# A convolutional FFN on one core: the first chunk's halves in the other order with x1 turned between them, the last group by pairs of blocks, the samples' halves summed by a product

## Chip, core and metric

The kernel runs on one core of one Trainium2 chip. The metric is the device time of one launch in microseconds (us): the kernel before has a median of 1758.8 us in 3 runs (1758.32 to 1759.49). The core has five engines with a static order of instructions each: TensorE (PE in the profile), VectorE (DVE), ScalarE (ACT), GpSimd (POOL) and SyncE (SP), which here issues most DMAs. An instruction waits on its engine until what it reads is there and what it overwrites is free; everything behind it on that engine waits too.

## What is computed

One layer of a hybrid decoder, for 256 tokens of a prompt and 64 tokens of 8 samples (8 each), D_MODEL = 2048, D_FF = 5632, all in float32:

```python
def decoder_layer(x, ssm_state, ssm_conv_state, ffn_conv_state, p):
    ...                                     # mix: chunk MLP and SSD, then w_out
    x = x + rms_norm(mix, p["norm_mix_post"])
    f, new_ffn_conv = conv_ffn(rms_norm(x, p["norm_ffn_pre"]), ffn_conv_state,
                               p["ffn_w_up"], p["ffn_conv_w"], p["ffn_conv_b"], p["ffn_w_down"])
    x = x + rms_norm(f, p["norm_ffn_post"])

def conv_ffn(h, conv_state, w_up, conv_w, conv_b, w_down):
    up = h @ w_up                           # 2048 -> 2 x 5632
    up, new_conv = causal_depthwise_conv(up, conv_state, conv_w, conv_b)   # 3 taps along the tokens
    g, u = jnp.split(up, 2, axis=-1)
    return (jax.nn.gelu(g, approximate=True) * u) @ w_down, new_conv
```

Only the FFN, its two norms and the last sum are touched. Below, x1 is x after the mix part and r3 is the reciprocal root of x1's mean square, one number for each token.

## The kernel before

**Layout.** Activations stand with features on the 128 partitions and the 320 tokens (256 prompt, 64 sample) as columns. TensorE multiplies in a rounded format, so every product of the prompt is made as three: high times high, weight's high times activation's low, weight's low times activation's high (L135 to L137 in the up-projection, L1465 in the down-projection). A group of weights (128x1024) is loaded by SP into `wraw`, ScalarE casts the high part `whi` (L124), VectorE subtracts for the low part `wlo` (L125); there are three buffers of each, so a cast waits until TensorE is done with an older one. For weights of the down-projection the lines are L1480 (cast) and L1481 (subtraction). The samples' rows of the down-projection are made with unsplit values (`pms`, `pds`, L1472).

**Up-projection.** It goes by NG = 11 groups g of 512 columns of the gate half (half 0) and 512 of the other half (half 1): `ffn_up(g)`. `project` runs 4 PSUM tiles of 128 columns over 16 feature blocks. Behind each tile stands `evac`: VectorE scales it by r3 into `pad` (L1334, L1335), ScalarE makes the first tap of the convolution (L1341), VectorE the other two (L1343), ScalarE gelu for half 0 (L1348), VectorE the product with the gate, `a` for the prompt and `a_s` for the samples (L1351, L1352). `Parts.cut` splits blocks of `a`, and sums of blocks (s1 to s4), into high (ScalarE, L398) and low (VectorE, L399) parts. Group 0 begins before r3 is known: `ps_one`, then `ps_other` are its last two tiles, and after a few of ps_one's products the token sums give r3 (L275 to L282), which TensorE spreads over all partitions (`spread`, L298) and ScalarE copies (L300).

**Down-projection.** The 512 rows of `w_down` that belong to group ck are chunk ck. `down_steps(ck)` is a generator that runs in the background of `ffn_up(ck+1)`: at each `yield` a slab of the up-projection goes on. For each half m of the 2048 output columns it makes seven products instead of eight (Strassen and Winograd's scheme; blocks b11, b12, b21, b22 of the weights, their sums t1 to t4 on POOL, L1510), each in a PSUM tile `pm` of 12 matmuls of 512 columns. `taken_in` then moves the tile to one of seven running sums per half: for chunk 0 by a ScalarE copy (L1457), later by a VectorE add (L1459). The sums of half 0 lie in `in_mix` (in the memory of x1, tag acc_mix), those of half 1 in `in_fp`. After chunk 9, `together(m)` adds the seven to the four blocks f that they stand for (L1555). The last chunk (10) is done by `down_plain` without the scheme (`pd`), some weights being held (`held_w`) for a second use; `others(n)` loads x1 back in rows of tokens (`load_x1`), `done` is `one_block` (square, and product with the norm's gain), and after a token block's four columns' blocks `whole` makes the root and the output (L1655 to L1687). Token blocks are c = 0 and 1 (prompt) and 2 (samples, whose columns lie in two halves on 128 partitions).

**x1 in rows.** The last sum needs x1 with tokens on partitions. `to_rows(i)`, called four times at the start of chunk 0, transposes a quarter of x1 in blocks of 32 on VectorE (L1440) and stores it by four DMAs on SP (L1443). Its buffers in_turn have the tags ohi and olo, which are also those of `a` and `s`. Since in_mix takes x1's memory, the first copy into in_mix comes after the four turns.

**Order.** A scheduler puts the instructions of each engine in a fixed order when the program is built: by the order of the code, by priorities (`first()` raises by 200000, weights by 100000) and by explicit `issue_after`.

## Time and profile before

| | us |
|---|---|
| median of 3 runs (lowest, highest) | 1758.8 (1758.32, 1759.49) |
| the profiled execution | 1760.49 |
| its span (first to last instruction) | 1758.8 |
| TensorE busy in it | 1728.8 (98%) |
| VectorE busy | 1355.5 (77%) |
| ScalarE busy | 881.2 (50%) |
| GpSimd busy | 692.6 (39%) |
| TensorE clock granted, mean | 0.992 |

The profile is of one execution; its clock is the share of full speed that TensorE was granted. In rows of the timeline the first number is the start, the second the duration in us; what stands in brackets is how long the instruction waited and for what. Rows of waits give the engine, the waiting tile and line, what ended the wait, then the total, the count and the longest. In rows by stretches each engine's busy time and count stand in the order TensorE, VectorE, ScalarE, GpSimd and SyncE, then the clock, the DMA engines' share and their GB/s.

### The profile page before, as it was taken

The page shows a single profiled execution, that of the slowest core. Times are in us where ns is not written, and L with a number is a line of the kernel's source. Part 1 is how long each engine was busy: PE and PEld are TensorE (multiplying, and loading weights), DVE is VectorE, ACT ScalarE, POOL GpSimd, SP SyncE. Part 2 cuts the span into 40 slices and gives each one's busy share as a digit, 9 for nine tenths or more (in the row PEclk, how much of TensorE's full clock was granted, in tenths as well). Part 3 has the DMA queues.
Part 4 walks back from the last instruction along what each step waited for, and adds up shares of the span by engine and source line. Part 5 has one row for each costly group of instructions (what it writes and reads, how often), then busy time and mean ns, then how long its engine had stood idle before and what let it go on. Part 6 is the DMA issues. An engine that isn't in the chain of part 4 may idle for free.

```text
span 1758.8 us, 29958 instructions
## 1 busy us (share of the span) xinstructions
PE 1728.8 (98%) x11221; PEld 1609.3 (92%) x11221; DVE 1355.5 (77%) x2127; ACT 881.2 (50%) x1276; POOL 692.6 (39%) x1006
## 2 busy tenths in 40 slices
PE   9999999999999999999989999999999999999986
PEld 9999999999999999999978898888888888888864
DVE  6549863657879787879867788879797979797885
ACT  6344544334656564645545444444444545454543
POOL 2432230000432324021345556565555556565534
PEclk9999999999999999999999999999999999999998
DMA  8776665555776677655665444455545454545442
GB/s 251 227 236 183 181 180 151 157 168 188 221 213 215 208 230 215 220 172 164 209 182 156 147 149 144 155 172 163 167 150 164 153 159 151 163 156 160 146 146 96
DMA packets 212962, 310.60 MB, mean 177 GB/s; under 512 B 22224, under 2 KB 112976, under 8 KB 212496
## 3 DMA queue, kind: packets, MB, share of 16 engines
q1 hardware_dynamic: 195424, 279.50, 52.0%
q0 software_dynamic: 6176, 13.87, 2.7%
q10 hardware_dynamic: 11216, 15.31, 2.5%
q8 instruction: 88, 1.44, 0.3%
q14 instruction: 58, 0.48, 0.1%
HBM read 285.00 MB, written 22.32 MB: 175 GB/s over the span
## 4 chain that ended last, share of the span: by engine, by line
PE 96%; DVE 2%; issue 1%; DMA 1%; ACT 0%; POOL 0%; DVEq 0%; ACTq 0%; SPq 0%; POOLq 0%
PE ps L135 20%; PE ps L137 20%; PE ps L136 20%; PE pm L1465 11%; PE pd L135 4%; PE pd L137 4%; PE pd L136 4%; PE pms L1472 4%; PE pd L1465 1%; PE y_ps L1088 1%; PE ps_v L135 1%; PE ps_v L136 1%; PE ps_v L137 1%; DVE wlo L125 0%; PE yo_ps L1003 0%
## 5 line engine op out<-in xcount | busy, mean ns | idle before, releaser
L135 PE MATMUL ps<-h_hi,whi 128*128 128x320 f32 x2428 | 750.1, 309 | 1.0 <-ACT whi L124 1.0
L137 PE MATMUL ps<-h_hi,wlo 128*128 128x320 f32 x2428 | 748.4, 309 | 0.5 <-DVE wlo L125 0.3
L136 PE MATMUL ps<-h_lo,whi 128*128 128x320 f32 x2428 | 748.5, 308 | 0.0
L125 DVE TENSOR_TENSOR wlo<-wraw,whi 128x1024 fp32r<-128x1024 f32 (+2 forms) x395 | 489.9, 1241 | 155.3 <-ACT whi L124 153.5
L124 ACT CAST whi<-wraw 128x1024 fp32r<-128x1024 f32 (+2 forms) x394 | 406.1, 1031 | 378.2 <-PE ps L136 139.9
L135 PEld LDWEIGHTS ps<-h_hi,whi 128*128 128x128 f32 x2428 | 455.8, 188 | 10.3 <-issue 1.3
L136 PEld LDWEIGHTS ps<-h_lo,whi 128*128 128x128 f32 x2428 | 456.0, 188 | 6.1
L137 PEld LDWEIGHTS ps<-h_hi,wlo 128*128 128x128 f32 x2428 | 455.5, 188 | 1.3 <-DVE wlo L125 1.3
L1481 DVE TENSOR_TENSOR wlo<-b,whi 128x1024 fp32r<-128x1024 f32 x120 | 153.8, 1281 | 79.7 <-ACT whi L1480 79.4
L1480 ACT CAST whi<-b 128x1024 fp32r<-128x1024 f32 x120 | 125.6, 1046 | 162.8 <-PE ps L136 153.8
L1510 POOL TENSOR_TENSOR b<-b,b 128x256 f32<-128x256 f32 x160 | 183.1, 1168 | 0.0
L135 PE MATMUL pd<-ohi,whi 128*128 128x320 f32 x448 | 138.7, 310 | 0.0
L137 PE MATMUL pd<-ohi,wlo 128*128 128x320 f32 x448 | 138.3, 309 | 0.0
L136 PE MATMUL pd<-olo,whi 128*128 128x320 f32 x448 | 138.3, 309 | 0.0
L1510 POOL TENSOR_TENSOR b<-b,t 128x256 f32<-128x256 f32 x80 | 75.0, 947 | 96.9 <-PE pms L1472 96.9
L1346 POOL COPY ptf<-pad 128x2 f32<-128x2 f32 x88 | 42.2, 480 | 166.9 <-DVE pad L1334 166.2
L1510 POOL TENSOR_TENSOR t<-b,b 128x256 f32<-128x256 f32 x80 | 89.7, 1151 | 23.3 <-DMA b<-in_ffn_w_down 16.1
L135 PEld LDWEIGHTS pd<-ohi,whi 128*128 128x128 f32 x448 | 84.1, 188 | 0.6
L136 PEld LDWEIGHTS pd<-olo,whi 128*128 128x128 f32 x448 | 84.1, 188 | 0.3
L137 PEld LDWEIGHTS pd<-ohi,wlo 128*128 128x128 f32 x448 | 84.1, 188 | 0.0
L248 DVE TENSOR_TENSOR acc_mix<-acc_mix,pd 128x320 f32<-128x320 f32 (+1 forms) x113 | 53.6, 477 | 28.0 <-PE pd L137 27.7
L1472 PE MATMUL pms<-b,a_s 128*64 128x512 f32 x320 | 73.1, 598 | 0.0
(407 smaller groups left out, 2496.1 us busy)
## 6 DMA issues: line engine op xcount, KB each, us to landing
wraw<-in_ffn_w_up SPq DMA_DIRECT2D x176, 512.0 KB, 4.5
wraw<-in_w_in SPq DMA_DIRECT2D x132, 512.0 KB, 3.9
b<-in_ffn_w_down SPq DMA_DIRECT2D x80, 512.0 KB, 4.5
wraw<-in_w_out SPq DMA_DIRECT2D x64, 512.0 KB, 3.5
st<-in_state_ssm SPq DMA_DIRECT2D x40, 256.0 KB, 4.3
out_ssm_state_sample<-st ACTq DMA_DIRECT2D x30, 256.0 KB, 2.6
cs<-dacs_d SPq DMA_DIRECT2D x16, 320.0 KB, 5.5
wraw<-in_w_in SPq DMA_DIRECT2D x12, 384.0 KB, 4.5
```

What stands on the lines that cost most here:

```text
L124: rounded[:] = [act.copy(hi, raw).ins]
L125: lowered[:] = [dve.tensor_tensor(out=lo, in0=raw, in1=hi.bitcast(F32), op=ALU.subtract).ins]
L135: pe.matmul(ps, whi, xhi, start=first, stop=False)
L136: pe.matmul(ps, whi, xlo, start=False, stop=False)
L137: last_made[0] = pe.matmul(ps, wlo, xhi, start=False, stop=last).ins
L248: added_last[:] = [dve.tensor_tensor(out=acc[:, nb, ts], in0=acc[:, nb, ts], in1=ps[:, ts], op=ALU.add).ins]
L1346: kept_rows[:] = [pool.tensor_copy(ptf[:, k, :], pad[:, 256:258]).ins]
L1465: last_made[0] = pe.matmul(ps, x[xi][:, k], w[wi][:, 512 * k:512 * k + 512], start=start and k + i == 0, stop=stop and k == 1 and i == 2).ins
L1472: last_made[0] = pe.matmul(ps[64 * h:64 * h + 64], a_s[:, k0 + k], w[h][:, 512 * k:512 * k + 512], start=start and k == 0, stop=stop and k ...
L1480: rounded[:] = [act.copy(hi, raw).ins]
L1481: dve.tensor_tensor(out=lo, in0=raw, in1=hi.bitcast(F32), op=ALU.subtract)
L1510: pool.tensor_tensor(out=to[:, cs], in0=raw[x][:, cs], in1=raw[y][:, cs], op=ALU.subtract)
```

## The change

It has three parts.

**First chunk.** For chunk 0 the halves go in the order m = 1, 0, and each half gets its room for sums (now of eight blocks, seven and the samples') when it begins: in_fp first. `to_rows` has buffers of its own (the tag that the norm's gain takes later) and is called behind products 1, 2, 7 and 3 of m = 1. Three yields stand ahead of the first product, as before.

**Last group.** In g = 10, half 1, the convolution after each tile is under `first()`, and the half is projected in two passes of 256 columns. Chunk 9 waits two yields more, so that four of its products, not two, stand behind the last product of the up-projection. `together(1)` is called one step of weights later.

**End.** The samples' sum of squares over both halves of partitions is made by a matmul with `pair` (ones where both halves meet, from two adds of `ident`), placed between the two parts of column block 2, instead of two DMAs and an add. Of the prompt, three blocks' sums are added ahead and the fourth goes into the root with these as its bias. VectorE multiplies by the gain in c = 0, blocks 2 and 3. ScalarE and GpSimd share the output only for c = 1, blocks 1 and 2. The gain is held as two tiles and loaded in two DMAs, gain_s later than before.

The diff, without the rewritten lines whose content the words above give:

```diff
             parts = Parts(a, a_s, g == NG - 1)
 
             def evac(half, j, ps):
+                with first() if g == NG - 1 and half == 1 else nullcontext():
+                    convolved(half, j, ps)
+
+            def convolved(half, j, ps):
...
-                for half in range(2):
-                    project(ffn_w_up, DFF * half + 512 * g, lambda j, ps: evac(half, j, ps))
+                project(ffn_w_up, 512 * g, lambda j, ps: evac(0, j, ps))
+                if g < NG - 1:
+                    project(ffn_w_up, DFF + 512 * g, lambda j, ps: evac(1, j, ps))
+                else:
+                    for h in range(2):
+                        project(ffn_w_up, DFF + 512 * g + 256 * h, lambda j, ps: evac(1, 2 * h + j, ps), width=256)
...
 
         def to_rows(i):
 
-            st = hp.tile([P, SN, 4, 32], F32, tag=("ohi", "olo")[i % 2], name="in_turn")
+            st = fp.tile([P, SN, 4, 32], F32, tag="gain", name="in_turn", bufs=2)
             dve.transpose(out=st, in_=x1[:, 4 * i:4 * i + 4].rearrange("p k (s f) -> p s k f", f=32))
...
-        sums_of_m, f_s = [], []
-
-        def room_for_sums():
-
-            in_mix = hp.tile([P, 9, 512], F32, tag="acc_mix", name="in_mix")
-            in_fp = fp.tile([P, 7, 512], F32, name="in_fp")
-            sums_of_m[:] = [[t[:, i] for i in range(7)] for t in (in_mix, in_fp)]
-            f_s[:] = [in_mix[:, 7 + m] for m in range(2)]
+        sums_of_m, f_s = [None, None], [None, None]
+
+        def room_for_sums(m):
+
+            room = fp.tile([P, 8, 512], F32, name="in_fp") if m else hp.tile([P, 8, 512], F32, tag="acc_mix", name="in_mix")
+            sums_of_m[m] = [room[:, i] for i in range(7)]
+            f_s[m] = room[:, 7]
...
 
             last_rows = kept_rows[0]
             if ck == 0:
-                for i in range(4):
-                    to_rows(i)
-                    if i in (0, 1):
-                        yield
-                room_for_sums()
-                yield
+                for _ in range(3):
+                    yield
             else:
-                yield
-                yield
-                if ck == NG - 2:
+                for _ in range(5 if ck == NG - 2 else 2):
                     yield
-            for m in range(2):
+            for m in (1, 0) if ck == 0 else (0, 1):
...
+                if ck == 0:
+                    room_for_sums(m)
...
                 for name in ("b11", "b12", "b22", "b21"):
                     load(name)
                 product(1, "a11", "b11")
+                if ck == 0 and m == 1:
+                    to_rows(0)
                 yield
...
                             later.append((nb, i, w))
                         others(n)
                         n += 1
-                        if n == 3:
+                        if n == 4:
                             together(1)
...
                 if i == 0:
                     ps = mm.tile([P, 512], F32, tag="mm", name=f"pd_{nb}_0")
                 prompt_products(ps, x_of_tokens(0, i), w, i == 0, i == 1, True)
+                if (nb, i) == (2, 0):
+                    between()
...
         def load_x1(n):
             with tc.issue_after(slab_load[-1]):
                 if n == 2:
+                    for h in range(2):
+                        sp.dma_start(gain_s[64 * h:64 * h + 64].rearrange("p (m e) -> p m e", m=2),
+                                     norm_last[0:1].rearrange("o (m h e) -> h o m e", m=2, h=2)[h].broadcast_to([64, 2, 512]))
...
+        pair = upper
+        for h in range(2):
+            dve.tensor_tensor(out=pair[:, 64 * h:64 * h + 64], in0=ident[:, :64], in1=ident[:, 64:], op=ALU.add)
+        most = {}
 
         def one_block(c, nb):
             t, g, _ = of(c, nb)
-            ends = c == 0 and nb == 3
-            with first() if ends else nullcontext():
+            by_vector = c == 0 and nb > 1
+            with first() if by_vector else nullcontext():
                 act.activation(unread, t, AF.Square, accum_out=squares[:, c, nb:nb + 1])
-                (dve if ends else pool).tensor_tensor(out=t, in0=t, in1=g, op=ALU.mult)
-            if nb == (1 if c == 2 else 3):
-                whole(c)
-
-        def whole(c):
+                (dve if by_vector else pool).tensor_tensor(out=t, in0=t, in1=g, op=ALU.mult)
+                if c < 2 and nb == 2:
+                    most[c] = fp.tile([P, 1], F32, name=f"most{c}")
+                    dve.tensor_reduce(out=most[c], in_=squares[:, c, :3], axis=mybir.AxisListType.X, op=ALU.add)
+                    dve.tensor_scalar(out=most[c], in0=most[c], scalar1=1.0 / D, scalar2=EPS, op0=ALU.mult, op1=ALU.add)
+            if c < 2 and nb == 3:
+                whole(c, squares[:, c, 3:4], most[c])
+            elif c == 2 and nb == 1:
+                with first():
+                    most[c] = fp.tile([P, 1], F32, name="most2")
+                    dve.tensor_reduce(out=most[c], in_=squares[:, c], axis=mybir.AxisListType.X, op=ALU.add)
+
+        def samples_summed():
+            ps = misc("both_halves")
+            with tc.issue_after(last_made[0]):
+                last_made[0] = pe.matmul(ps[:, 0:1], pair, most[2], start=True, stop=True).ins
+            whole(2, ps[:, 0:1], eps)
+
+        def whole(c, some, others):
             with first():
-                ss, v, s, r, n = (fp.tile([P, 1], F32, name=f"last_{i}{c}") for i in "uvsrn")
-                dve.tensor_reduce(out=ss, in_=squares[:, c], axis=mybir.AxisListType.X, op=ALU.add)
-                if c == 2:
-                    other = fp.tile([P, 1], F32, name="last_o")
-                    for h in range(2):
-                        sp.dma_start(other[64 - 64 * h:P - 64 * h], ss[64 * h:64 * h + 64])
-                    dve.tensor_tensor(out=ss, in0=ss, in1=other, op=ALU.add)
-                act.activation(s, ss, AF.Sqrt, scale=1.0 / D, bias=eps)
-                dve.tensor_scalar(out=v, in0=ss, scalar1=1.0 / D, scalar2=EPS, op0=ALU.mult, op1=ALU.add)
+                v, s, r, n = (fp.tile([P, 1], F32, name=f"last_{i}{c}") for i in "vsrn")
+                act.activation(s, some, AF.Sqrt, scale=1.0 / D, bias=others)
+                dve.tensor_scalar(out=v, in0=some, scalar1=1.0 / D, scalar2=others, op0=ALU.mult, op1=ALU.add)
                 dve.reciprocal(v, v)
                 dve.tensor_tensor(out=r, in0=s, in1=v, op=ALU.mult)
                 dve.scalar_tensor_tensor(out=n, in0=s, scalar=-0.5, in1=r, op0=ALU.mult, op1=ALU.mult)
                 dve.scalar_tensor_tensor(out=r, in0=n, scalar=1.5, in1=r, op0=ALU.add, op1=ALU.mult)
                 for nb in range(2 if c == 2 else 4):
                     t, _, y = of(c, nb)
-                    by_two = nb == (0, 2, 0)[c] or (c, nb) == (1, 1)
+                    by_two = c == 1 and nb in (1, 2)
                     if by_two:
                         act.activation(t, t, AF.Copy, scale=r)
                         pool.tensor_tensor(out=y, in0=t, in1=y, op=ALU.add)
                     else:
                         dve.scalar_tensor_tensor(out=y, in0=t, scalar=r, in1=y, op0=ALU.mult, op1=ALU.add)
                     if c < 2:
-                        (act if by_two else sp).dma_start(o_y[P * c:P * c + P, 512 * nb:512 * nb + 512], y)
+                        (act if by_two or c == 0 and nb % 2 else sp).dma_start(o_y[P * c:P * c + P, 512 * nb:512 * nb + 512], y)
...
```

What it moves, as the program of each engine is written before and after (engine's operation, tile written, tiles read; a count at a row's end stands for that many alike).

VectorE in group 0 around the steps that lead to r3 (sq is the sum of squares, rs_* the root's steps, in_turn a turn of x1, the last row the first use of r3), before:

```order
L1303 TENSOR_TENSOR sq_9170<-sq_two 128x320
L125 TENSOR_TENSOR wlo<-wraw,whi 128x1024
L275 TENSOR_SCALAR rs_v<-tsum 128x3
L279 RECIPROCAL rs_r<-rs_s 128x3
L280 SCALAR_TENSOR_TENSOR rs_t<-rs_v,rs_r 128x3
L281 TENSOR_TENSOR rs_t<-rs_t,rs_r 128x3
L282 SCALAR_TENSOR_TENSOR rs_r<-rs_t,rs_r 128x3
L125 TENSOR_TENSOR wlo<-wraw,whi 128x1024
L1334 TENSOR_TENSOR pad<-ps_0_9175,r_9643 128x256
```

and after:

```order
L1303 TENSOR_TENSOR sq_9170<-sq_two 128x320
L1448 STREAM_TRANSPOSE in_turn<-acc_mix 128x1280
L125 TENSOR_TENSOR wlo<-wraw,whi 128x1024
L275 TENSOR_SCALAR rs_v<-tsum 128x3
L1448 STREAM_TRANSPOSE in_turn<-acc_mix 128x1280
L279 RECIPROCAL rs_r<-rs_s 128x3
L125 TENSOR_TENSOR wlo<-wraw,whi 128x1024
L280 SCALAR_TENSOR_TENSOR rs_t<-rs_v,rs_r 128x3
L281 TENSOR_TENSOR rs_t<-rs_t,rs_r 128x3
L282 SCALAR_TENSOR_TENSOR rs_r<-rs_t,rs_r 128x3
L1338 TENSOR_TENSOR pad<-ps_0_9175,r_9643 128x256
```

Two turns and a subtraction that stood elsewhere now stand among these steps, and the subtraction behind them stands ahead of the last three. On TensorE the spread of r3 stands 28 products of ps_one behind the token sums, where 9 stood.

ScalarE in group 1, where chunk 0's first results are copied out, before:

```order
L1480 CAST whi<-b_10088 128x1024
L1457 COPY in_mix<-pm 128x512
L1457 COPY in_mix<-pms 128x512
L1457 COPY in_mix<-pm 128x512 x2
L124 CAST whi<-wraw 128x1024
L1457 COPY in_mix<-pm 128x512
L1480 CAST whi<-b_10094 128x1024
L1457 COPY in_mix<-pm 128x512
L124 CAST whi<-wraw 128x1024
```

and after:

```order
L124 CAST whi<-wraw 128x1024
L1487 CAST whi<-b_10067 128x1024
L124 CAST whi<-wraw 128x1024
L1464 COPY in_fp<-pm 128x512
L398 CAST a_hi<-a 128x256 x2
L398 CAST s_hi<-s 128x256
L1487 CAST whi<-t_10117 128x1024
L398 CAST s_hi<-s 128x256 x2
L1464 COPY in_fp<-pms 128x512
L124 CAST whi<-wraw 128x1024
L1464 COPY in_fp<-pm 128x512
```

The copies into in_mix stood in a row; those into in_fp stand one at a time between casts. On TensorE, 72 products of the up-projection and then 18 of chunk 0 stood there in a row; now 24 and 6 alternate.

VectorE in group 10, from the last convolutions to chunk 9's last products, before:

```order
L1351 TENSOR_TENSOR a<-ucv,gcv 128x256
L125 TENSOR_TENSOR wlo<-wraw,whi 128x1024
L1459 TENSOR_TENSOR in_fp<-in_fp,pm 128x512 x2
L125 TENSOR_TENSOR held_w<-wraw,held_w 128x1024
L125 TENSOR_TENSOR wlo<-wraw,whi 128x1024
L125 TENSOR_TENSOR held_w<-raw,held_w 128x1024
L125 TENSOR_TENSOR wlo<-raw,whi 128x1024
L1352 TENSOR_TENSOR a_s<-ucv,gcv 128x64
L1343 SCALAR_TENSOR_TENSOR ucv<-pad,prm,ucv 128x336
L1555 TENSOR_TENSOR in_fp<-in_fp 128x512
L1343 SCALAR_TENSOR_TENSOR ucv<-pad,prm,ucv 128x336 x2
L1351 TENSOR_TENSOR a<-ucv,gcv 128x256
```

and after:

```order
L1488 TENSOR_TENSOR wlo<-b_18343,whi 128x1024
L1347 SCALAR_TENSOR_TENSOR ucv<-pad,prm,ucv 128x336 x4
L1355 TENSOR_TENSOR a<-ucv,gcv 128x256
L1356 TENSOR_TENSOR a_s<-ucv,gcv 128x64
L1466 TENSOR_TENSOR in_fp<-in_fp,pm 128x512
L1355 TENSOR_TENSOR a<-ucv,gcv 128x256
L1356 TENSOR_TENSOR a_s<-ucv,gcv 128x64
L1466 TENSOR_TENSOR in_fp<-in_fp,pm 128x512
L399 TENSOR_TENSOR a_lo<-a,a_hi 128x256
L1466 TENSOR_TENSOR in_fp<-in_fp,pm 128x512
L1488 TENSOR_TENSOR wlo<-b_18349,whi 128x1024
L125 TENSOR_TENSOR wlo<-wraw,whi 128x1024
```

The subtraction in the last row but one (of b_18349, the weights of product 4 in half 1) is now behind the last convolutions, products and cuts, where subtractions stood ahead of them. On TensorE 24 products of chunk 9 stand behind the last of the up-projection; 12 did.

More of the change, by code (lines that the diff above doesn't have):

```diff
@@ L1536, in down_steps @@
                 product(7, "s3", "t3")
+                if ck == 0 and m == 1:
+                    to_rows(2)
                 yield
@@ L1564, in together, with down_plain @@
                 f[c][2 * m + n] = t[i]
-        def down_plain(ck, parts, done, others):
+        def down_plain(ck, parts, done, others, between):
             def x_of_tokens(c, i):
@@ L1614, in hybrid_step @@
         pool.memset(squares, 0.0)
-        gain = fp.tile([P, D], F32, name="gain")
-        gain_s = fp.tile([P, 1024], F32, name="gain_s")
+        gain = []
         for g in range(1, NG):
```

17 lines of the change are left out of this document (11 added, 6 removed).

## Prediction

> **What bounds the kernel now.** I read the page first (engines' shares and the chain that ended last), then TensorE's waits, then the granted clock in short stretches around each wait, then the timeline there. Page:
>
> ```profile
> PE 1728.8 (98%) x11221; PEld 1609.3 (92%) x11221; DVE 1355.5 (77%) x2127; ACT 881.2 (50%) x1276; POOL 692.6 (39%) x1006
> PE 96%; DVE 2%; issue 1%; DMA 1%; ACT 0%; POOL 0%; DVEq 0%; ACTq 0%; SPq 0%; POOLq 0%
> ```
>
> TensorE is busy for 98% and nearly is the chain. The edit removes no product, so only the 30 us in which TensorE stands, and what follows from them, can move. The waits for a named engine (us, times, longest):
>
> ```profile
> PE pd L1465 <- ACT a_hi L398: 8.3, 1, 8.3
> PE pm L1465 <- ACT in_mix L1457: 5.1, 1, 5.1
> PE ps L135 <- ACT whi L124: 1.0, 1, 1.0
> PE ps L137 <- DVE wlo L125: 0.3, 1, 0.3
> ```
>
> The second to fourth lie in the first chunk of the down-projection, the first lies ahead of the last chunk. In the timeline of TensorE (start, duration):
>
> ```profile
> 901.45 0.31 PE L136 MATMUL ps<-h_lo,whi 128*128 128x320 f32 x1
> 901.59 0.31 PE L137 MATMUL ps<-h_hi,wlo 128*128 128x320 f32 x1
> 907.02 0.80 PE L1465 MATMUL pm<-whi,s_hi 128*128 128x512 f32 x1 [5.11 <-ACT in_mix L1457]
> ...
> 911.42 0.39 PE L1465 MATMUL pm<-whi,s_lo 128*128 128x512 f32 x1
> ...
> 1702.66 0.40 PE L1465 MATMUL pm<-whi,a_lo 128*128 128x512 f32 x1
> 1702.89 0.40 PE L1465 MATMUL pm<-wlo,a_hi 128*128 128x512 f32 x1
> 1711.55 0.80 PE L1465 MATMUL pd<-whi,a_hi 128*128 128x512 f32 x1 [8.26 <-ACT a_hi L398]
> ...
> 1716.92 0.39 PE L1465 MATMUL pd<-held_w,a_hi 128*128 128x512 f32 x1
> ...
> 1744.52 0.39 PE L1465 MATMUL pd<-kept,a_hi 128*128 128x512 f32 x1
> ```
>
> Products of 320 columns start 0.15 apart, those of 512 columns 0.23. So TensorE stands from 901.74 to 907.02 (5.3) and from 1703.12 to 1711.55 (8.4), and is done at 1744.75. After each gap it is slow: ten products take 907.02 to 911.42 = 4.4, where ten times 0.23 is 2.3 (2.1 lost), and twelve take 1711.55 to 1716.92 = 5.4 for 2.8 (2.6 lost). The granted clock says why (stretch; the column before "DMA share" is the clock):
>
> ```profile
> 904.50:905.00 0.50, 0.00 (x0) 0.00 (x0) 0.17 (x1) 0.00 (x0) 0.00 (x0) 0.53 0.00 0
> 911.00:911.50 0.50, 0.50 (x3) 0.41 (x2) 0.50 (x1) 0.09 (x1) 0.50 (x1) 0.64 0.00 0
> 1706.50:1707.00 0.50, 0.00 (x0) 0.00 (x0) 0.50 (x1) 0.50 (x1) 0.00 (x0) 0.67 0.97 369
> 1716.50:1717.00 0.50, 0.50 (x3) 0.41 (x2) 0.50 (x2) 0.21 (x1) 0.00 (x0) 0.59 0.00 0
> 1747.00:1748.00 1.00, 0.00 (x0) 0.00 (x0) 1.00 (x2) 0.48 (x1) 0.44 (x1) 0.81 0.00 0
> ```
>
> Between 1.0 and 0.5 these put the falls at 904.53, 1706.67 and 1747.62, the rises at 911.36 and 1716.91. They lie 2, 3 and 12 steps of 3.41 us apart: the clock changes only on such a grid. Before the first fall TensorE had been busy for 0.6 of the step.
>
> Before the change, then, the first chunk loses 1.0 + 0.3 + 5.3 + 2.1 = 8.7, the last gap 8.4 + 2.6 = 11.0, and the end runs 14 us past TensorE.
>
> **Part 1, first chunk.** The products' results get the free room in_fp first, so the copies that sat behind the four turns of x1 (wait of 5.1) no longer do, and the bunch of three late products spreads out: 8.7 goes. What is late next: two turns now stand ahead of r3 on VectorE.
>
> ```profile
> 846.11 0.49 DVE L1303 TENSOR_TENSOR sq<-sq_two 128x320 f32<-128x320 f32 x1
> 846.51 1.22 DVE L125 TENSOR_TENSOR wlo<-wraw,whi 128x1024 fp32r<-128x1024 f32 x1
> ...
> 848.68 0.16 DVE L282 SCALAR_TENSOR_TENSOR rs_r<-rs_t,rs_r 128x3 f32<-128x3 f32 x1
> ...
> 851.15 0.41 DVE L1334 TENSOR_TENSOR pad<-ps,r 128x256 f32<-128x256 f32 x1
> ...
> 880.34 2.89 DVE L1440 STREAM_TRANSPOSE in_turn<-acc_mix 128x1280 f32<-128x1280 f32 x2
> ```
>
> ```profile
> 848.99 0.51 PE L298 MATMUL spread<-ident,rs_r 128*128 128x128 f32 x3
> 852.86 0.31 PE L135 MATMUL ps_other<-h_hi,whi 128*128 128x320 f32 x1
> 849.86 0.42 ACT L300 COPY r<-spread 128x320 f32<-128x320 f32 x1
> ```
>
> By the new order: turn 846.5 to 847.9 (2.89 for two), subtraction to 849.1, the small one, turn to 850.7, reciprocal, subtraction to 852.0, three small steps: r3 at 852.6, where it was 848.84. On TensorE the spread stands 19 products (2.8 us) later, so TensorE reaches it at 851.6 and waits 1.1. ScalarE's copy then ends at 853.8, the first pad at 854.4 frees the PSUM tile of ps_other, which begins at 854.5, not 852.86: **+1.6**. Behind that I followed VectorE's new order to the end of the first half with these durations; the low part of the second half's first weights comes out 0.4 us ahead of TensorE, so **+0.3** for spots as narrow. Bounds of part 1: 0 and 8.7 - 1.6 - 0.3 - 2.1 (a wait that lowers the clock) = 4.7 to 8.7 gained; I take 6.8, the row-by-row sum.
>
> The samples' rooms, 16 store issues and gain's bytes stay the same in number, the gain in two halves; they lie on SP beside full TensorE. The two adds that make `pair` (64 columns, under the 0.16 row) stand between subtractions hundreds of us before use. Both at nothing.
>
> **Part 2, last group.** TensorE's work is the same, but 24 products of 512 columns, not 12, follow the last up-projection (end H), and convolutions go ahead of weight subtractions on VectorE. Rows that carry it:
>
> ```profile
> 1702.65 1.36 DVE L1459 TENSOR_TENSOR in_fp<-in_fp,pm 128x512 f32<-128x512 f32 x2
> ...
> 1709.69 1.03 DVE L1343 SCALAR_TENSOR_TENSOR ucv<-pad,prm,ucv 128x336 f32<-128x336 f32 x2
> 1710.65 0.41 DVE L1351 TENSOR_TENSOR a<-ucv,gcv 128x256 f32<-128x256 f32 x1
> 1710.98 0.21 DVE L1352 TENSOR_TENSOR a_s<-ucv,gcv 128x64 f32<-128x64 f32 x1
> ...
> 1711.60 0.75 DVE L399 TENSOR_TENSOR a_lo<-a,a_hi 128x256 fp32r<-128x256 f32 x2
> ```
>
> ```profile
> 1701.38 1.04 ACT L124 CAST held_w<-wraw 128x1024 fp32r<-128x1024 f32 x1
> ...
> 1702.33 1.04 ACT L124 CAST whi<-wraw 128x1024 fp32r<-128x1024 f32 x1
> ```
>
> The plain products' operands a11 and a21 are now cut long before: the 8.4 wait is gone as such. But the fourth product's low weights stand on VectorE behind the last two blocks' convolution. ScalarE casts the third product's weights from H + 0.1 (its buffer frees at H), VectorE's low part is out at H + 2.35; then ucv four times 0.48 (to 4.3), a and a_s 0.47 (4.75), a sum 0.6, a and a_s (5.8), a sum (6.4); a_lo needs a_hi, which on ScalarE stands behind two activations and four casts 0.95 apart (H + 6.5): to 6.9; a sum (7.5); the low part itself 1.15: H + 8.7. TensorE wants it two products into the fourth: H + 3 x 1.39 + 0.46 = 4.6. So TensorE waits **4.2** there. Queued behind: the plain part's own low weights, out before the wait's product is over, and on SP the load into that raw buffer (b21) with six more; their users come over 10 us later. Bounds: 0 (if the order's late place did not bite) and 5.5 (casts at twice their step). Does the clock fall? A gap of 4.2 puts 2.8 or more idle into some step of 3.41 for two thirds of its positions, and the step that fell had 2.8. So likelier yes, at 2.1 to 2.6; I take 2.1, the shorter gap's row. New loss 6.3, gain **4.7**; ends 11.0 (no wait) and 11.0 - 5.5 - 2.6 = 2.9.
>
> The Trainium skill, page "TensorE: Matmul & The Clock Gate", Part 1, says the clock halves after an idle window of about 3.4 us and that the windows run freely. The grid above agrees. By its wording, a wholly idle window, a gap of 4.2 would do it in a quarter of its positions only and the sum would be 2.1 lower.
>
> **Part 3, the end.**
>
> ```profile
> 1743.22 0.63 ACT L1655 ACTIVATE unread<-in_mix 128x512 f32<-128x512 f32 x1 [4.00 <-DVE last_v L1670]
> ```
>
> ```profile
> 1747.50 0.68 DVE L1459 TENSOR_TENSOR in_fp<-in_fp,pd 128x512 f32<-128x512 f32 x1
> ...
> 1751.46 2.42 DVE L1682 SCALAR_TENSOR_TENSOR x_tok<-in_fp,last_r,x_tok 128x512 f32<-128x512 f32 x2
> ```
>
> The last block is taken in 2.75 after TensorE's end, since VectorE is still at the samples, whose root stood behind two squares on a ScalarE that was held till 1743.2. After: the samples' root comes ahead of the squares (0.5 earlier on balance, since VectorE takes over a samples' block, a gain and a sum of its own), the sum of squares is three quarters done (0.65), four output blocks on VectorE alone end about 0.4 sooner than with a 1.75 one among them, and the product of both halves costs TensorE 0.25 (a product of one column, between others; bounds 0 and 0.5). The DMA pair it replaces was not what held the end. Sum **-1.3**; bounds: nothing, if ScalarE is held as long and VectorE's order only trades places, and 3.5, if the last block is taken in at once.
>
> **Sum.** 8.7 - 1.6 - 0.3 + 4.7 + 1.3 = 12.8. The profiled execution's span of 1758.8 becomes 1746.0, its time of 1760.49 becomes 1747.7. The runs without profile have a median of 1758.8, 1.7 below the profiled time, so I give 1746.0.
>
> **Rivals.**
> - The clock stays up across the 4.2 gap (falls on the grid's third position): 1746.0 - 2.1 = 1743.9. For it: the grid runs free of the program. 18%.
> - No wait at the fourth product, since VectorE's steps overlap better than their rows: 1746.0 - 6.3 = 1739.7. Against it: the order is fixed and every row in it measured. 10%.
> - The first chunk starves TensorE: a turn needs its buffer's four stores on SP, which stand behind weight loads that wait for VectorE. A 3 us gap with a lowered clock costs 4.5: 1750.5. For it: VectorE's narrowest margin there is 0.4. 17%.
> - Savings are eaten and nothing measurable (0.2% = 3.5 us is about what a measurement can tell from no change) is left: both of the last losses together with the end's bound of nothing and the wait's upper end, 1755 and above. 7%.
> - Slower: the first turn's memory was that of stored states, and by the order it waits for those stores on POOL's queue, with r3 behind it on VectorE.
>
> ```profile
> L1173 POOL DMA_DIRECT2D out_ssm_state_prompt<-s x1: 539/539/539, 835.3 to 835.3; - x1
> ...
> DMA to landing us min/median/max: 5.9/7.2/7.4
> ```
>
> They land by 843, the turn is due at 846.5. Only a landing after 859.3 (24 us, three times the longest) would eat 12.8; at 863 it gives 1762.5. 3%.
>
> **Numbers.** The forecast has 45%. The range from 1741 to 1752 leaves out the case without a wait, and the last two; it takes in the rest with their bounds. Faster by over 0.2%: 45 + 18 + 10 + 17 = 90%; within: 7%; slower: 3%.
>
> **What would show it.** Right: no wait of pm for in_mix; the spread waiting about 1 us and ps_other starting some 1.6 after it did; one wait of about 4 us, of pm for the low weights (wlo) of the last product before pd, with the clock at 0.5 behind it; pd without a wait for a_hi; from TensorE's end to the span's end 12.5 to 13 us. Wrong: a wait of several us for weights around the first chunk, a wait of pd, or an end as long as before.

## The result, and the profile after

The changed kernel has a median of 1750.25 us in 4 runs (1749.75 to 1750.71), the one before 1759.14 in 4 (1758.32 to 1760.14): a ratio of 0.9949, 95% interval 0.9932 to 0.9966. It is faster, by 8.9 us. The profiled execution took 1750.16, its span 1748.4. The page, engines and chain:

```profile
PE 1727.3 (99%) x11223; PEld 1606.9 (92%) x11223; DVE 1365.8 (78%) x2133; ACT 880.1 (50%) x1274; POOL 694.9 (40%) x1003
PE 94%; DVE 3%; POOL 2%; issue 1%; ACT 0%; DVEq 0%; ACTq 0%; POOLq 0%
```

TensorE's waits for a named engine (total, times, longest; L1472 is the product that was L1465, L1488 the low part of a product's weights that was L1481):

```profile
PE pm L1472 <- DVE wlo L1488: 5.1, 3, 4.1
PE ps L137 <- DVE wlo L125: 1.3, 2, 1.0
...
PE ps_other L135 <- DVE pad L1339: 0.5, 1, 0.5
```

The waits for in_mix (5.1) and for a_hi (8.3) are gone. What stands in their place, in TensorE's timeline (start, duration, in brackets the wait):

```profile
853.02 0.38 PE L135 MATMUL ps_other<-h_hi,whi 128*128 128x320 f32 x1 [0.51 <-DVE pad L1339]
...
1652.67 0.50 PE L1472 MATMUL pm<-wlo,s_hi 128*128 128x512 f32 x1 [0.57 <-DVE wlo L1488]
...
1659.45 0.42 PE L137 MATMUL ps<-h_hi,wlo 128*128 128x320 f32 x1 [0.23 <-DVE wlo L125]
...
1673.75 1.07 PE L1479 MATMUL pms<-b,a_s 128*64 128x512 f32 x2
1675.24 0.49 PE L1472 MATMUL pm<-wlo,a_hi 128*128 128x512 f32 x1 [0.42 <-DVE wlo L1488]
...
1679.51 3.65 PE L1479 MATMUL pms<-b,a_s 128*64 128x512 f32 x14
...
1697.44 0.40 PE L1472 MATMUL pm<-whi,a_lo 128*128 128x512 f32 x1
1701.91 0.71 PE L1472 MATMUL pm<-wlo,a_hi 128*128 128x512 f32 x1 [4.07 <-DVE wlo L1488]
...
1735.12 0.39 PE L1472 MATMUL pd<-kept,a_hi 128*128 128x512 f32 x1
```

The 4.07 is the forecast's wait at the fourth product. The rows from 1652 to 1679, of chunk 9's products and group 10's up-projection, were not in it. VectorE at the fourth product, and the clock (the column before the DMA share):

```profile
1698.98 0.21 DVE L1356 TENSOR_TENSOR a_s<-ucv,gcv 128x64 f32<-128x64 f32 x1
1699.12 0.67 DVE L1466 TENSOR_TENSOR in_fp<-in_fp,pm 128x512 f32<-128x512 f32 x1
1699.71 0.41 DVE L399 TENSOR_TENSOR a_lo<-a,a_hi 128x256 fp32r<-128x256 f32 x1
1700.05 0.67 DVE L1466 TENSOR_TENSOR in_fp<-in_fp,pm 128x512 f32<-128x512 f32 x1
1700.65 1.21 DVE L1488 TENSOR_TENSOR wlo<-b,whi 128x1024 fp32r<-128x1024 f32 x1
```

```profile
1705.00:1705.50 0.50, 0.50 (x3) 0.40 (x2) 0.50 (x2) 0.00 (x0) 0.00 (x0) 0.55 0.94 328
```

VectorE has no gap there; the low part comes last in a row of convolutions, products, sums and a cut. The clock is low for one step of 3.41 us on the prediction's grid, which ends at 1705.45; at half speed that costs half a step, 1.7. TensorE ends at 1735.35 (before: 1744.75) and the span 13.05 later (before: 14.05). The wait at the fourth product came as told; what was paid between 1650 and 1680 the forecast did not have.

### The profile page after: what moved, and what is told of

It is laid out like the page before. It is cut to its first block, busy times and chain, and to the rows that moved or that the text cites. A ratio compares the mean times of both kernels' runs of the same rounds, so it can differ in the third digit from the quotient of the medians.

```text
span 1748.4 us, 29947 instructions
## 1 busy us (share of the span) xinstructions
PE 1727.3 (99%) x11223; PEld 1606.9 (92%) x11223; DVE 1365.8 (78%) x2133; ACT 880.1 (50%) x1274; POOL 694.9 (40%) x1003
## 4 chain that ended last, share of the span: by engine, by line
PE 94%; DVE 3%; POOL 2%; issue 1%; ACT 0%; DVEq 0%; ACTq 0%; POOLq 0%
PE ps L135 20%; PE ps L137 20%; PE ps L136 20%; PE pm L1472 10%; PE pd L135 4%; PE pd L136 4%; PE pd L137 4%; PE pms L1479 3%; POOL b L1513 1%; PE pd L1472 1%; PE y_ps L1088 1%; PE ps_v L136 1%; PE ps_v L135 1%; PE ps_v L137 1%; DVE wlo L1488 1%
## 5 line engine op out<-in xcount | busy, mean ns | idle before, releaser
L125 DVE TENSOR_TENSOR wlo<-wraw,whi 128x1024 fp32r<-128x1024 f32 (+2 forms) x395 | 490.1, 1242 | 146.3 <-ACT whi L124 144.3
L1488 DVE TENSOR_TENSOR wlo<-b,whi 128x1024 fp32r<-128x1024 f32 x120 | 154.0, 1284 | 77.2 <-ACT whi L1487 76.0
L1513 POOL TENSOR_TENSOR b<-b,t 128x256 f32<-128x256 f32 x80 | 78.6, 992 | 69.9 <-PE pms L1479 67.5
```

Of the source, the lines that this page charges most:

```text
L125: lowered[:] = [dve.tensor_tensor(out=lo, in0=raw, in1=hi.bitcast(F32), op=ALU.subtract).ins]
L1488: dve.tensor_tensor(out=lo, in0=raw, in1=hi.bitcast(F32), op=ALU.subtract)
L1513: pool.tensor_tensor(out=to[:, cs], in0=raw[x][:, cs], in1=raw[y][:, cs], op=ALU.subtract)
```

## Experiments

Each was run against the kernel before in its own batch (medians of before: 1759.8, 1759.9, 1759.3, 1760.3, 1760.1); intervals are 95% ones, of the ratio. The batches' medians of before differ by up to 1.0, so times from different batches are compared no closer than that.

**The three parts alone.** First chunk alone, with the rooms that it needs:

```diff
-                    to_rows(i)
...
+            for m in (1, 0) if ck == 0 else (0, 1):
...
+                if ck == 0 and m == 1:
+                    to_rows(0)
```

> Part 1 alone (with the room it needs, the gain in two tiles and gain_s loaded late), last group and end as before. My theory: the losses add up stage by stage, so here the 8.7 us of the first chunk go, 0.7 come back at the spread and ps_other and 1.0 at a low part behind the third turn, and nothing changes in group 10: about 7 us below the kernel before, 1752, no wait of pm for in_mix, and the last gap (pd for a_hi, 8 us) as before. Rival: part 1 also makes the three small waits of group 10 (through the moved rooms or the other order of the halves): then two waits for low weights between 1650 and 1676 us show here and the gain is 3.6.

1753.33, ratio 0.9961 (0.9948 to 0.9973): 6.5 us (7 expected). Its waits:

```profile
PE pd L1464 <- ACT a_hi L398: 8.6, 1, 8.6
...
PE ps L137 <- DVE wlo L125: 1.0, 1, 1.0
PE ps_other L135 <- DVE pad L1335: 0.5, 1, 0.5
```

The two small waits of the first chunk are there, those between 1650 and 1676 are not: they are not of this part. Last group alone:

```diff
+                with first() if g == NG - 1 and half == 1 else nullcontext():
+                    convolved(half, j, ps)
...
+                for _ in range(5 if ck == NG - 2 else 2):
```

> Part 2 alone. My theory: the last gap falls from 11.0 to 5.9 us (one wait of 4 us of pm for the low weights of the fourth product, the clock at 0.5 behind it for 1.7), but group 10 gets about 3.4 us of small waits, all of TensorE for low weights that stand on VectorE behind convolutions: about 1.7 us below the kernel before, 1757. Rival: the small waits are not of this part, and it gives the 5 us of the forecast, 1754.

1757.96, ratio 0.9990 (0.9981 to 0.9999): 1.8 us, not the prediction's 4.7.

```profile
PE pm L1473 <- ACT in_mix L1465: 4.7, 1, 4.7
PE pm L1473 <- DVE wlo L1489: 4.6, 2, 4.1
...
PE ps L137 <- DVE wlo L125: 0.5, 2, 0.3
```

The wait of 4.1 and the small ones come with this part. The end alone (`both_halves`, `most`, the output's split):

```diff
...
+                if (nb, i) == (2, 0):
+                    between()
...
```

> Part 3 alone. My theory: TensorE's end stays within 0.3 us (the product of both halves costs 0.25), and the stretch from there to the end of the span falls from 14.05 to about 13.0: 1 us below the kernel before, 1758. Rival: the end is set by when VectorE takes in the last block, which needs the shorter last gap of part 2 too; then the stretch stays at 14 and the time is the same within 0.3.

1759.12, ratio 0.9996 (0.9987 to 1.0004): 0.7 us, which the interval does not tell from nothing; in its trace TensorE ends at 1744.93 and the span 13.2 later, 0.9 less than before. The three medians add up to 9.0, the whole change gives 8.9.

**Is it that subtraction's place, or VectorE's work?** Chunk 9's weights of half 1 ahead of the convolutions:

```diff
...
-                with tc.high_priority(offset=100000), tc.issue_after(rounded[0]):
+                with tc.high_priority(offset=300000 if ck == NG - 2 and m else 100000), tc.issue_after(rounded[0]):
...
```

> The changed kernel, with the high and low parts of chunk 9's weights of half 1 put ahead of the convolutions on ScalarE and VectorE. My theory: behind the last up-projection VectorE's work, not its order, is the bound: the wait of 4.1 us for the fourth product's low weights goes, 0.8 comes at the third product, and 4 us come one step later, as a wait of pd for the low part of the first plain weights (L125), so that this place gains nothing; but the samples' products no longer split the first product at 1673, and that gives 1.7 us: 1748 to 1749 where the changed kernel has 1750.2. Rival: the wait is only that one subtraction's place; it goes with nothing in its stead, the clock stays up, and 4.1 + 1.7 + 1.7 = 7.5 us are gained, 1742.7.

1752.48, ratio 0.9955 (0.9941 to 0.9968): no better than the changed kernel, and above the 1748 to 1749 expected.

```profile
PE pd L1472 <- DVE wlo L125: 4.2, 1, 4.2
PE ps L137 <- DVE wlo L125: 1.9, 3, 1.1
```

The 4.1 is now a 4.2 of pd, one step later, as expected: behind the last up-projection VectorE has more to do than TensorE's products cover. The gain of 1.7 at 1673 did not come: the two sample products still stood apart, now ahead of a wait of ps for L125. The clock stayed low longer, too (the slow spacing of 0.43 from 1704.85 to 1710.3).

**Which convolutions need to be first?** Only the second pass's, then none:

```diff
-                with first() if g == NG - 1 and half == 1 else nullcontext():
+                with first() if g == NG - 1 and half == 1 and j > 1 else nullcontext():
```

> The changed kernel, but only the second pass's convolutions (blocks 2 and 3 of half 1 of group 10) stand ahead of the rest; those of the first pass have their ordinary place again. My theory: the 1.7 us at 1673 (two sample products drawn into the first product, since its low weights stood behind the first pass's convolutions) go; behind the last up-projection VectorE's work is the same, so a wait of 3.5 to 4.2 us stays there, at the third or the fourth product: 1748 to 1748.5 where the changed kernel has 1750.2. Rival: the split of the sample products comes from the two passes or the later yields and stays: 1750.

1749.12, ratio 0.9940 (0.9928 to 0.9953). The sixteen sample products stand in a row again, and TensorE ends 1.7 earlier than in the changed kernel. The wait at the end has broken up:

```profile
PE pm L1472 <- DVE wlo L1488: 2.4, 2, 1.9
PE pm L1472 <- ACT whi L1487: 1.4, 2, 0.8
```

So the split at 1673 needs the first pass's priority. The wait of 3.5 to 4.2 expected at one product came as three, of 0.6, 0.8 and 1.9. With none first (`nullcontext()` alone):

> The changed kernel without any priority for the convolutions of group 10. My theory: the wait at 1673 goes (1.7), the fourth product's weights wait 0.5 to 1.5 us; but the last convolutions now stand behind five low parts of the plain weights, two of which wait for transfers, and pd waits some 7 us for a_hi or a_lo of the second half of the rows, with the clock lowered behind it: about 1754, 4 us above the changed kernel. Rival: convolutions first is the whole cause of the remaining wait, and without it the four products hide everything: 1743.

1751.70, ratio 0.9955 (0.9943 to 0.9968). The direction held, the sizes did not: 1.5 us above the changed kernel for 4, with a wait of 3.8 for 7.

```profile
PE pd L1472 <- ACT a_hi L398: 3.8, 1, 3.8
PE pm L1472 <- DVE wlo L1488: 1.5, 3, 0.6
```

The low parts that I had waiting for transfers did not wait, so pd went on at 1709.5, not 1714. The waits at 1652 and 1659 stayed in both: they are not of the priority.

**Less work for VectorE.** On top of the kernel with chunk 9's weights first: the first plain weights first too, the low parts of the second and third on GpSimd:

```diff
...
-                        slab(rows_of(ffn_w_down, 4 * ck + 2 * i, 2, 512 * nb, 512), kept=kept, room=raw)
+                        with tc.high_priority(offset=300000 if n < 1 else 0):
+                            slab(rows_of(ffn_w_down, 4 * ck + 2 * i, 2, 512 * nb, 512), kept=kept, room=raw, by=pool if n in (1, 2) else None)
...
```

> As the kernel with chunk 9's weights of half 1 first, and besides the first plain weights first too, and the low parts of the second and third plain weights on GpSimd, which stands idle there: 2.4 us of work are taken from VectorE in that stretch. My theory (VectorE's work is the bound there): no wait over 0.6 us between the last up-projection and the first sample products of the plain part, the clock stays up; 0.4 at the third product stays: 1744 to 1745. Rival: order alone or work alone does not matter, since GpSimd slows VectorE (low parts took 1.75 us beside its sums, 1.21 alone) and takes 2.7 us or more for each: a wait of 2 to 3 us of pd for held_w or for a_lo, the clock down again: 1749.

1750.06, ratio 0.9947 (0.9933 to 0.9960): nothing gained. That is about the rival's time (1749), and its cause, that GpSimd slows VectorE; but the waits came at other places than it named. GpSimd, then VectorE, in the same stretch:

```profile
1698.09 2.54 POOL L125 TENSOR_TENSOR held_w<-wraw,held_w 128x1024 fp32r<-128x1024 f32 x1 [1.94 <-ACT held_w L124]
1700.58 2.58 POOL L125 TENSOR_TENSOR wlo<-wraw,whi 128x1024 fp32r<-128x1024 f32 x1
```

```profile
1698.28 2.63 DVE L1355 TENSOR_TENSOR a<-ucv,gcv 128x256 f32<-128x256 f32 x1
1700.83 2.42 DVE L1356 TENSOR_TENSOR a_s<-ucv,gcv 128x64 f32<-128x64 f32 x1
```

The products a and a_s, 0.41 and 0.21 us in the changed kernel at this place, ended 0.3 and 0.1 us after GpSimd's subtractions, not before. The wait of 4 is gone from TensorE, but 4.4 us were added to VectorE for the 2.4 taken away, and came out further on:

```profile
PE both_halves L1693 <- DVE most L1688: 2.4, 1, 2.4
...
PE pds L1479 <- DVE in_fp L1466: 1.4, 1, 1.4
```

The new product of both halves stands in TensorE's row and waits there for the samples' sum, with all that is behind it; the clock fell behind that wait. The same with the turns held behind r3 and only the second pass first:

```diff
+            with tc.issue_after(rsqrt_ins[-1]):
+                dve.transpose(out=st, ...)
```

> As the one before, with only the second pass's convolutions first, and with the turns of x1 held behind r3's root on VectorE. My theory: besides the gain of the one before, the 1.2 us left at 1675 go, and in the first chunk the spread and ps_other lose their 0.9 and the low part behind the third turn its 1.2: 1741 to 1742. Rival: turns behind r3 press on the next low weights, and a wait of 1 to 2 us comes back at ps between 855 and 890: 1743 to 1744.

1749.98, ratio 0.9947 (0.9935 to 0.9960), where 1741 to 1742 were expected. The gaps at spread and ps_other went (0.9), but in the same chunk a low part was late by 1.7 in place of 1.0, with smaller ones beside it, and the wait of both_halves stayed:

```profile
PE both_halves L1693 <- DVE most L1688: 2.1, 1, 2.1
PE ps L137 <- DVE wlo L125: 1.9, 2, 1.7
```

**Two products behind, not four.** The yields alone set back, the rest of the changed kernel kept:

```diff
-                for _ in range(5 if ck == NG - 2 else 2):
+                for _ in range(3 if ck == NG - 2 else 2):
```

> The changed kernel, but chunk 9 begins where it did before the change, so that two of its products, not four, stand behind the last product of the up-projection; convolutions first and the two passes stay. My theory: the later begin costs more than it hides. The waits at 1652 and 1659 (1.2) go with it, the sample products stay whole (1.5), and VectorE has the last products' low parts done before the last convolutions; by its order the first plain weights' low part is out 6.4 us behind the last up-projection, wanted after 3.3: one wait of 3 us of pd for L125, with the clock at half speed for a step (1.7): 1746 to 1747 where the changed kernel has 1750.2. Rival: four products are what hides the cut of the last group; with two pd waits 5 us or more for a_hi or L125, and the small waits stay, since they come from the passes or the priority: 1750 to 1752.

1748.81, ratio 0.9932 (0.9919 to 0.9946), above the 1746 to 1747 expected; the profiled execution took 1746.63. Its waits, the end of the longest, and the clock behind it:

```profile
PE ps L137 <- DVE wlo L125: 2.9, 2, 1.8
PE pd L1472 <- DVE wlo L125: 2.2, 1, 2.2
```

```profile
1697.19 0.40 PE L1472 MATMUL pd<-whi,a_lo 128*128 128x512 f32 x1
1699.82 0.49 PE L1472 MATMUL pd<-wlo,a_hi 128*128 128x512 f32 x1 [2.23 <-DVE wlo L125]
```

```profile
1701.00:1701.50 0.50, 0.50 (x4) 0.41 (x3) 0.50 (x2) 0.00 (x0) 0.00 (x0) 0.85 0.97 393
```

The waits at 1652 and 1659 and the split are gone, so the later yields made the first two and had a part in the third; a wait of ps of 1.8 at 1679, for a low part that stands on VectorE behind the first pass's convolutions, is new. The last wait is 2.2 (expected 3). The five runs took 1745.14 at a mean clock of 0.998, 1746.63 at 0.996 and 1748.81 to 1749.19 at 0.995. Only that of 1746.63 has a trace, with one low step, 1701.35 to 1704.77; that the others had none and two of them is my reading of their clocks, not shown.

**By need.** All low parts on VectorE, in the order in which TensorE meets them:

```diff
-                lowered[:] = [dve.tensor_tensor(out=lo, in0=raw, in1=hi.bitcast(F32), op=ALU.subtract).ins]
+                with tc.high_priority(offset=300000) if soon else nullcontext(), tc.issue_after(lowered[0]) if soon else nullcontext():
+                    lowered[:] = [dve.tensor_tensor(out=lo, in0=raw, in1=hi.bitcast(F32), op=ALU.subtract).ins]
...
+            with tc.issue_after(lowered[0]) if i == 3 else nullcontext():
+                dve.transpose(out=st, ...)
...
-                if (nb, i) == (2, 0):
+                if (nb, i) == (2, 1):
```

(`soon` is set for the first two plain weights; the weights of chunk 9's half 1 are first as in the fourth experiment.)

> As the kernel with low parts on GpSimd, but all of them on VectorE again, in the order in which TensorE needs them: the third and fourth products' low parts, the first and the second plain weights', then the last convolutions; the product of both halves one half block later, behind (2,1); and the fourth turn of x1 behind the low part that it pressed on. My theory: with nothing on GpSimd VectorE's steps keep their short times (0.41 and 0.21 us for a and a_s, where they took 2.6 and 2.4 beside GpSimd), so the backlog is 3.3 us smaller; no wait over 0.6 between the last up-projection and TensorE's end, the clock up, the wait of 1.2 at 889 gone; TensorE done 6 us earlier than in the changed kernel, the end 12.5 to 13 us behind it: 1743.5 to 1745. Rival: the backlog only travels on, to the samples' sum or the cut of the second rows, and a wait of 2 us or more with a lowered clock shows there: 1748 or more.

1746.08, ratio 0.9922 (0.9908 to 0.9936), 1 us above the 1743.5 to 1745 expected. VectorE's steps are short again and the longest wait is 1.0 (0.6 expected):

```profile
1699.39 0.42 DVE L1356 TENSOR_TENSOR a<-ucv,gcv 128x256 f32<-128x256 f32 x1
1699.73 0.22 DVE L1357 TENSOR_TENSOR a_s<-ucv,gcv 128x64 f32<-128x64 f32 x1
```

```profile
PE ps L138 <- DVE wlo L126: 1.4, 3, 0.7
...
PE pd L1474 <- DVE wlo L126: 1.0, 1, 1.0
```

No wait of this kernel lowered the clock. TensorE ends at 1730.88, 4.5 earlier than in the changed kernel, but the end follows 14.0 later and not 12.5 to 13, which loses 1 us of it again. With the product of both halves at its old place:

```diff
-                if (nb, i) == (2, 1):
+                if (nb, i) == (2, 0):
```

> The same with the product of both halves where the changed kernel has it, behind (2,0). My theory: the samples' sum is ready at about 1726 us, 1 us behind the place where TensorE meets this product, so a wait of 0.5 to 1.5 us of both_halves comes, too short to lower the clock for sure: 0.5 to 1.5 us above the one before. Rival: the sum is ready early enough once GpSimd is free, and both are the same within 0.3.

1746.52, ratio 0.9925 (0.9913 to 0.9938). The wait came, with 0.8:

```profile
PE both_halves L1694 <- DVE most L1689: 0.8, 1, 0.8
```

Its price, 0.4 between the medians of one batch, is inside the intervals. At last the tail, from the kernel with the later sum:

```diff
-            with first():
+            with first() if c < 2 else nullcontext():
...
-                    by_two = c == 1 and nb in (1, 2)
+                    by_two = False
```

> As the kernel by need with the later sum, but the second prompt block's output is made by VectorE alone (GpSimd and ScalarE no longer share it), and the samples' output steps have no priority over taking in the last block. My theory: beside GpSimd two of VectorE's output steps took 1.84 and 1.70 us for 0.75 alone, so four on VectorE alone cost no more than those two; the last block is taken in some 0.7 to 1.5 us earlier: the stretch behind TensorE's end falls from 14.0 to about 13: 1745 to 1745.5. Rival: the end is bound by the chain of the last block (add, square, root, four outputs, store) and by when VectorE comes free from the samples, whose work is unchanged: within 0.4 us, 1746.

1745.59, ratio 0.9917 (0.9903 to 0.9930), the lowest, though its step against 1746.08, from another batch, is no more than the intervals allow. The end follows TensorE's by 12.8 us (1731.43 to 1744.2; 13 expected). One output step still stood beside GpSimd:

```profile
1726.01 1.29 POOL L1679 TENSOR_TENSOR in_fp<-in_fp,gain_s 128x512 f32<-128x512 f32 x1 [0.48 <-ACT unread L1678]
1726.03 1.82 DVE L1713 SCALAR_TENSOR_TENSOR x_tok<-in_mix,last_r,x_tok 128x512 f32<-128x512 f32 x1
...
1727.84 0.73 DVE L1713 SCALAR_TENSOR_TENSOR x_tok<-in_mix,last_r,x_tok 128x512 f32<-128x512 f32 x1
```

## Why the prediction was right, and where it was not

The sign and the range were right; the number was 4.3 too low. Four stretches of TensorE's timeline, each from the start of one product to the start of another, show where (us, profiled executions):

| | before | after | gained | forecast |
|---|---|---|---|---|
| ps_one's first product to group 10's first | 775.2 | 767.8 | 7.4 | 6.8 |
| group 10, first to last up-projection | 80.4 | 81.0 | -3.4 | 0 |
| from there to TensorE's last product | 44.3 | 42.2 | 4.9 | 4.45 |
| TensorE's end to the end of the span | 14.0 | 13.1 | 1.0 | 1.55 |

Twelve products of 512 columns (2.8 us at 0.23 each) moved from the second stretch to the third, and the gains allow for that. The forecast's 0.25 for the product of both halves, which it took off part 3, lies in the third. The four add up to 9.9, where 12.8 were forecast. The spans differ by 10.4; the other 0.5 lies ahead of 51 us, where the first product of tile ps starts at 51.3 before and at 50.8 after. From there to ps_one it is 793.3 us in both, and in the other kernels' traces that first product starts between 50.1 and 51.5, so this half microsecond is not of the change.

- First chunk: 6.8 forecast. Alone it gave 6.5, by the trace of the changed kernel 7.4. The 8.7 went, and with it 0.3 at a spot at 892.9 that the prediction's list had not; 1.7 came back, of which 0.7 at spread and ps_other (forecast 1.6: the turn began at 844.7 and not at 846.5, because the new order had one low part less ahead of it), and 1.0 at a narrow spot (forecast 0.3).

```profile
887.49 1.50 DVE L1448 STREAM_TRANSPOSE in_turn<-acc_mix 128x1280 f32<-128x1280 f32 x1
888.14 4.79 POOL L1513 TENSOR_TENSOR b<-b,b 128x256 f32<-128x256 f32 x4
888.92 1.74 DVE L125 TENSOR_TENSOR wlo<-wraw,whi 128x1024 fp32r<-128x1024 f32 x1
```

  There the low part stood behind the fourth turn and took 1.74 beside GpSimd's sums, where the forecast had 1.22. The last experiments, which put that turn one low part later, have no wait at 889 and 0.5 at 900. That the part came out near its forecast is in part luck: one item too large by 0.9 and one too small by 0.7.
- Wait at the fourth product: forecast 4.2, measured 4.07; the low part was out 8.9 after the last up-projection (forecast 8.7). The clock fell, as taken, and cost 1.7, not 2.1. The gain at this wait was 5.1, not 4.7. The two thirds of the grid's positions come out of the prediction's own numbers as six tenths.
- **The step that failed** is the first sentence on part 2, that TensorE's work is the same, read as if only the place behind the last up-projection counted. The order was followed from there on, not through group 10 ahead of it. There the change cost 3.4: 0.8 at 1652, 0.5 at 1659, 0.1 at 1657, and 1.9 where two sample products were drawn in ahead of a waiting product. Before, the sixteen stood in a row:

```profile
1677.00 3.65 PE L1472 MATMUL pms<-b,a_s 128*64 128x512 f32 x16
```

  After, two of them hold 1.49 us (1673.75 to 1675.24) for 0.45 of work, the other fourteen take as long as the sixteen did, and the rest are the slower starts behind each break. The same stretch in the other traces tells what made it:

| group 10, first to last up-projection | us | cost against before |
|---|---|---|
| before | 80.39 | |
| first chunk alone | 80.39 | 0 |
| last group alone | 80.61 | 3.0 |
| the changed kernel | 81.02 | 3.4 |
| only the second pass first | 79.12 | 1.5 |
| none first | 79.11 | 1.5 |
| two products behind, all first | 82.52 | 2.1 |
| by need, later sum | 81.09 | 3.5 |

  (The rows but for the first two and the one with two products behind hold 2.8 less of chunk 9's products, which the cost adds.) So the cost is of part 2; 1.5 of it comes with the later yields, whatever the priority, and 1.9 needs the first pass's priority as well. With the yields set back, priority and passes make one wait of 1.8 instead. The kernel by need still pays 3.5; it gains 0.9 in the first chunk and 4.1 behind the last up-projection.
- End: forecast 1.3 with the product of both halves at 0.25; by the trace 1.0, less 0.2 for that product; alone 0.7, with an interval that takes in nothing.
- From the spans to the medians: these differ by 8.9 and not by 10.4, since the profiled execution of before was 1.35 above its median and that of after was not. The forecast had taken 1.7 off for such a difference. So of the 4.3, 2.9 is the sum of the parts and 1.8 is this step; the half microsecond ahead of 51 us works against them.
- Rivals: the clock did not stay up, the wait was there, no 3 us gap came in the first chunk, and the first turn did not wait for the state's stores. The first rival had less room than it was given: from group 0 to TensorE's end, the clock fell behind every wait of 2.1 us or more in these traces; the shortest was that for both_halves with the turns held. The third's 4.5 for a gap of 3 would, with the 1.7 to 2.1 that a low clock cost here, have been 4.7 to 5.1.

What stays open is how much of the last experiment's 0.5 is the order and how much chance. Neither the yields set back (2.1 in place of 3.5 in group 10) nor the second pass alone first (1.5) was tried together with the order by need.

## What to carry to other kernels

A priority that lifts one kind of work, or a later start of another, is paid by all that it passes, in the whole stretch where it holds, so follow the waiting engine's order through all of that stretch. When a wait moves instead of going, add up the feeding engine's work up to the point where it is needed: if that exceeds the time, only less work or an order by need helps, and work handed to GpSimd may come back as time on VectorE. A small product in TensorE's row that reads a late scalar holds everything behind it, so place it where the scalar has long been ready.

## What the hardware showed

While GpSimd ran an elementwise instruction on two tiles, VectorE's instructions that read two tiles from the on-chip memory (SBUF) did not end before it: 2.63 for 0.41 and 2.42 for 0.21 us beside 2.54 and 2.58, and 1.82 for 0.73 beside 1.29. An add that reads one of its operands from PSUM, TensorE's output memory, was not held (pds is such a tile):

```profile
1722.82 2.70 POOL L1679 TENSOR_TENSOR in_fp<-in_fp,gain 128x512 f32<-128x512 f32 x2 [4.70 <-ACT unread L1678]
1724.51 0.67 DVE L1468 TENSOR_TENSOR in_fp<-in_fp,pds 128x512 f32<-128x512 f32 x1
```

The Trainium skill, page "SBUF — State Buffer", section "SBUF: two separate sides", says that the two engines share a pair of ports, which is a lock that the one that comes first keeps for the whole instruction. The rows agree, to the end of each instruction.

The clock did not need a step of the grid without any work. It fell in the changed kernel behind a step in which TensorE stood for 3.3 of 3.41 us (1698.62 to 1701.91; the step ends at 1702.03), and in the kernel with two products behind after one in which it stood for 1.9: the step began at 1697.94, TensorE went on at 1699.82, and the clock fell at 1701.35. So the prediction's second reading, of a wholly idle window, does not hold here, and its 2.8 is no least value. The wait of 1.8 at 1679 in that same execution left the clock up.
